# Attention on one core: which VectorE step a cast on GpSimd is tied to, small memsets in front of casts, and a new order of the work

## The chip, the core and the metric

The kernel runs on one core of a Trainium2 chip. The metric is the device time of one execution in microseconds (us). The time before is the median of three runs, 115.96 us (115.36 to 116.09). The engines have short names in the profile: PE is TensorE's matmul, PEld its weight load, DVE is VectorE, ACT is ScalarE, POOL is GpSimd, SP is SyncE, which here only issues DMAs.

## The reference

Softmax attention over 8 batches and 8 heads, 512 queries and keys, 64 columns each, in float32:

```python
q, k, v: (8, 8, 512, 64) float32
scores = einsum('bhqd,bhkd->bhqk', q, k) / sqrt(64)
attn = exp(scores - scores.max(-1)); attn = attn / attn.sum(-1)
return einsum('bhqk,bhkd->bhqd', attn, v)
```

## The kernel before, in words

**The pieces.** Two heads make a pair g (32 pairs, 0 to 31). Three float32 tiles of a pair (q, k and v, 128 partitions by 512 elements, 256 KB each) are loaded by DMA from SP's queue (line 462) into seven buffers of each kind. GpSimd casts each tile to float16: k and q into the tile `qkp` (line 478, five buffers), v into one of twelve tiles `vp` (line 468), which hold a column of ones beside the 64 columns so that the last matmul also gives the row sums. TensorE transposes `qkp` into PSUM (line 502, eight transposes for a pair), and VectorE copies the result to `tqk` in SBUF (line 515). Pairs 0 and 1 go other ways at the start (`first_pair`, and lines 475 to 477 and 508 to 512).

**The groups.** The scores of two blocks of 128 keys by 512 queries make a group m: two matmuls (line 542) into one of three PSUM tiles `st` of 128 by 1024. There are 128 groups, and the last of them is done in two halves. Most groups go to ScalarE, which takes the exponential in one ACTIVATE from `st` to `pt` (line 546). Sixteen groups, listed in `Plan.ON_DVE`, get their exponential on VectorE instead, in six steps: `raise_` (line 566) reads `st` from PSUM and writes a 16-bit whole number `pd`; then five passes in SBUF follow, `pass_` 0 to 4: `m<-pd` (line 583), `pe<-pd` (line 592), the product `m<-m` (line 600), `m<-m` (line 602), and the product `pd<-pd,m` (line 606). The exponential of such a group is the sum of two float16 parts, `pe` and `pd`; TensorE takes the sum in the values' matmuls, which use both as weights.

**The values.** `values` (line 638) multiplies the exponentials by `vp` into a PSUM tile `o` of seven columns of 128 queries each. When a tile is full, VectorE takes the reciprocal of the sums (line 612, `reciprocal`, the plan's step "rec") and multiplies (line 617, `normalise`, the plan's "mul") into a ring in SBUF, from which SP stores (line 628). `last_values` and `finish` end the last head (lines 654, 667, 668, 674).

**Who sets the order.** Each engine works through its own queue in order. Which instruction stands where in each queue is decided before the kernel is built, by the class `Plan`: a small model steps through time, five nanoseconds a step, and for each of PE, DVE, POOL and SP picks the next step by fixed durations and rules. `run` returns the steps sorted by time, and the kernel issues them in that order. The chip is not told of the times; it only sees the order and the semaphores. Rules that matter here:

- `due` (lines 79 to 91) sorts the casts: those of k and q are due `DUEK` before a pair's scores, that of v `DUEV` after them (and `DUEL` later still where a group of the pair is on VectorE). The same order gives the first loads, and a load of pair g+7 follows the cast of pair g.
- `step_pool` (line 118) emits a cast when no pass is at work, or when its due time less `PRE` has come. `step_dve` (line 290) emits casts in front of a VectorE step that is not a pass: up to two before a raise, one before a copy or a normalise, none before a reciprocal. `emit` (line 101) writes the cast down, and from 9000 on (`CALM`) with the flag that it is to be tied.
- Tied means: `cast_behind` (line 489) makes the cast wait on a semaphore for the VectorE instruction that was issued last (`latest[0]`). The steps that `dve` (line 485) records are the raise, the passes, the copy, the reciprocal and the normalise.
- `self.port` is the model's idea of an SBUF port that GpSimd's casts and VectorE's passes share: a pass may not start while a cast holds it (`CAST_PORT`), and a cast not while a pass runs.
- `LATE_NORM`, `LATE_COPY` and `LATE_MUL` bound how far a pass may put off a step of VectorE that will soon be ready; `HURRY`, `SOON` and `BACKLOG` say when PE turns to scores or waits for a PSUM tile, by how much work ScalarE still has.

**Waits of a cast.** A cast of k or q also waits for its DMA, and the one that comes first into a reused `qkp` (the cast of k) for the transposes on TensorE that read the buffer five pairs earlier. An instruction carries few waits; further ones stand before it as instructions of their own in GpSimd's queue.

Of the kernel before, what the change touches and what calls it, by code (L numbers as in the profile page):

```python
# [9 lines left out]
FP32 = mybir.dt.float32  # L10
# [7 lines left out]
class Plan:  # L18
# [15 lines left out]
    STEP = 5  # L34
    CALM, KEEN = 9000, 4
    FIRST_UNIT = 4
    ON_DVE = (5, 9, 19, 22, 35, 40, 50, 53, 63, 73, 78, 85, 92, 100, 109, 120)

    LATE_NORM, LATE_COPY, HURRY, SOON, BACKLOG = 600, 2400, 800, 280, 300
    LATE_MUL, WAIT = 2000, 200  # L40
    SLACK, AHEAD = 0, 2

    CAST, CAST_PORT, CAST_DONE, TO_POOL = 557, 475, 130, 150
    FIRST_LAND, LOAD, STORE, LATENCY, ISSUE = 5200, 740, 370, 2300, 470
    QUEUED, URGENT = 3500, 16
    RAW, QK16, NV, NU = 7, 5, 12, 112
    PAIR, DUEK, DUEV, DUEL, PRE = 3300, 4050, 6000, 6000, 500

    def __init__(self, groups, pairs, first):
        self.groups, self.pairs = groups, pairs  # L50
# [47 lines left out]
    def note(self, t, *what):  # L98
        self.steps.append((t, len(self.steps)) + what)

    def emit(self, t, after):
        _, g, n = self.uncast.pop(0)
        shared = (g, n) == (1, "q")
        self.note(t, "cast", g, n, t > self.CALM)
        if not shared:
            self.casts.append((g, n, t if after is None else after + self.TO_POOL))
        if g + self.RAW < self.pairs:
            self.loads.append((g + self.RAW, n))
# [9 lines left out]
    def step_pool(self, t):  # L118
        if self.uncast and self.uncast[0][1:] != (1, "q") and not self.casts and self.pool <= t:
            quiet = not self.passes and self.port <= t and not any(x[1] == "raise" for x in self.ready)  # L120
            if self.fits(t) and (quiet or self.uncast[0][0] - self.PRE < t):
                self.emit(t, None)
        if self.casts and self.pool <= t and self.port <= t:
            g, n, after = self.casts[0]
            if after <= t and self.landed.get((g, n), 1e9) <= t:
                self.casts.pop(0)
                self.pool = t + self.CAST
                self.port = t + self.CAST_PORT
                self.cast_done[(g, n)] = t + self.CAST + self.CAST_DONE

    def step_sp(self, t):
        if self.sp > t or self.dma > t + self.QUEUED:
# [157 lines left out]
    def step_dve(self, t):  # L290
        if self.uncast and self.uncast[0][1:] == (1, "q"):
            if self.landed.get((1, "q"), 1e9) <= t:
                self.emit(t, None)
                self.dve = t + 240
                self.pool = self.port = t + 330
                self.cast_done[(1, "q")] = t + 400
            return
# [7 lines left out]
        if now:  # L305
# [5 lines left out]
            _, kind, what = job  # L311
            slots = {"raise": 2, "rec": 0}.get(kind, 1)
            while slots and not self.casts and self.fits(t, 60 if slots == 1 else 0):
                self.emit(t, self.dve_done if self.dve_done > t - 300 else None)
                slots -= 1
                if slots and self.fits(t, 500):
                    self.emit(t, self.dve_done if self.dve_done > t - 300 else None)
                    slots -= 1
            self.note(t, kind, *what)
            if kind == "rec":  # L320
# [14 lines left out]
            else:  # L335
# [2 lines left out]
                self.raised.add(what[0])  # L338
                self.passes += [(what[0], s) for s in range(len(self.PASSES))]
                self.passed[what[0], None] = self.dve + self.PASS_DONE  # L340
            self.dve_done = self.dve
        elif self.passes and self.port <= t:
            able = [x for x in self.passes if self.passed.get((x[0], self.NEEDS[x[1]]), 1e9) <= t]
            if not able:
                return
            m, s = able[0]
            end = t + self.PASSES[s]
            late = {
                "copy": self.LATE_COPY,
                "rec": self.LATE_NORM,  # L350
                "mul": self.LATE_MUL,
                "raise": self.LATE_NORM,
                "finish": 0,
            }
            full = len(self.raised) == self.BITS
            if all(x[0] > end - late[x[1]] or (full and x[1] == "raise") for x in self.ready):
                self.passes.remove((m, s))
                self.note(t, "pass", m, s)
                self.dve = self.port = self.dve_done = end
                self.passed[m, s] = end + self.PASS_DONE  # L360
                if s == len(self.PASSES) - 1:
                    self.raised.remove(m)
                    self.exps[m] = end + self.PASS_DONE + self.TO_PE + self.SLACK

    def run(self):
        t = 4600
        self.dve_done = 0
        while self.m < len(self.groups) or self.todo or self.head or self.ready or self.passes or self.stores or self.last_part < 4:
            self.step_sp(t)
            self.step_pool(t)  # L370
# [11 lines left out]
def kernel(  # L382
# [97 lines left out]


    latest = []
    SYNC = mybir.DependencyInfo(mybir.DependencyClass.Sync, mybir.DependencyReason.DATA)

    def dve(ins):
        latest[:] = [ins]
        return ins

    def cast_behind(g, name, behind):
        ins = cast(g, name)  # L490
        if behind and latest:
            tc.add_manual_dep(ins.ins, latest[0].ins.name, SYNC, reason="SBUF ports")

    def transposes(g, n, bank):
        if n == 0:
# [3 lines left out]
            tps[g] = ps_x.tile([P, 2, NI, P], FP16, tag=f"x{bank ^ n}", name=f"tp_{g}_{n}")  # L499
        n = 1 - n  # L500
        for i in range(NI):
            nc.tensor.transpose(tps[g][:, n, i, :], qkp[g][:, n, i, :], ident)  # L502
        if g == 1 and n == 1:
            copy(g, n)

# [328 lines left out]
```

## Time and profile before

| what | value |
|---|---|
| median of three runs | 115.96 us |
| the profiled execution | 115.99 us |
| span of its instructions | 114.2 us |
| granted TensorE clock | 0.998 |
| busy PE / DVE / ACT / POOL | 104.4 / 103.3 / 106.5 / 56.8 us |
| instructions PE / DVE / ACT / POOL | 1687 / 226 / 118 / 101 |
| read and written in HBM | 25.17 MB, 8.39 MB |

The span runs from the first to the last instruction; the 1.8 us between it and the time of the execution lie around it. A group line of the profile gives line, engine, operation, written and read tiles, shapes and count, then busy time and the mean duration of one, then the idle time before. In a timeline a row is start, duration, engine, line, operation, tiles, count; neighbours of one kind are merged into one row. Durations of neighbours on one engine overlap, since the next instruction is taken up while the last one finishes. So an engine's pace is read from start to start.

### The profile page before, as it was taken

How to read it: one execution, taken by the hardware profiler on the slowest of the kernel's cores; microseconds unless marked ns; L12 is line 12 of the kernel's file. 1: busy time of each engine (PE TensorE's matmuls, PEld its weight loads, DVE VectorE, ACT ScalarE, POOL GpSimd, SP SyncE). 2: the span in 40 equal slices, each digit the busy share in tenths (PEclk: the TensorE clock that was granted, in tenths of full speed). 3: DMA queues.
4: the chain of work that ended last, by engine and by line, in shares of the span. 5: the costliest groups of instructions: out<-in, count | busy, mean ns of one | idle time of the engine just before them, and what ended most of it. 6: DMA issues, size and time to landing. Idle time of an engine off the chain costs nothing.

```text
span 114.2 us, 4337 instructions
## 1 busy us (share of the span) xinstructions
PE 104.4 (91%) x1687; PEld 67.9 (59%) x1687; DVE 103.3 (90%) x226; ACT 106.5 (93%) x118; POOL 56.8 (50%) x101
## 2 busy tenths in 40 slices
PE   7966999999999889999999999999999999999950
PEld 2623566566856457666658557567675676577640
DVE  1557899999999999999999999999999999999660
ACT  4698999999999999999999999999999999999940
POOL 2156844785445744784473675655828374400000
PEclk9999999999999999999999999999999999999999
DMA  2899999999999999789899999999995993755243
GB/s 94 277 359 379 384 386 375 384 380 378 384 354 350 354 375 354 259 268 302 216 374 361 305 277 329 326 350 349 366 322 165 301 291 121 260 182 187 98 149 130
DMA packets 35381, 33.84 MB, mean 296 GB/s; under 512 B 2592, under 2 KB 35360, under 8 KB 35360
## 3 DMA queue, kind: packets, MB, share of 16 engines
q1 hardware_dynamic: 34928, 33.17, 87.3%
q10 hardware_dynamic: 432, 0.39, 1.0%
q8 instruction: 13, 0.21, 0.8%
q14 instruction: 8, 0.07, 0.2%
HBM read 25.17 MB, written 8.39 MB: 294 GB/s over the span
## 4 chain that ended last, share of the span: by engine, by line
DVE 50%; PE 20%; DMA 11%; ACT 9%; issue 4%; POOL 1%; SPq 1%; ACTq 0%
PE o L638 10%; DVE pd L566 10%; DVE tqk L515 10%; DVE ring L617 9%; ACT pt L546 9%; PE st L542 8%; DVE m L600 5%; DMA q<-in_q_dram 5%; DVE pd L606 4%; DMA out_dram<-ring 4%; DVE pe L592 3%; DMA v<-in_v_dram 3%; DVE rc L612 2%; DVE m L602 2%; DVE m L583 2%
## 5 line engine op out<-in xcount | busy, mean ns | idle before, releaser
L546 ACT ACTIVATE pt<-st 128x1024 f16<-128x1024 f32 (+1 forms) x110 | 101.3, 1054 | 0.7 <-PE st L542 0.3
L638 PEld LDWEIGHTS <-pt 128*128 128x128 f16 x880 | 38.7, 98 | 13.0 <-issue 10.6
L638 PE MATMUL o<-vp,pt 128*128 128x65 f16 x880 | 45.5, 194 | 0.7 <-DVE ring L617 0.2
L542 PE MATMUL st<-tqk 64*128 64x512 f16 (+1 forms) x250 | 42.5, 381 | 2.2 <-ACT pt L546 0.7
L478 POOL CAST qkp<-k 128x512 f16<-128x512 f32 x31 | 19.1, 616 | 16.5 <-DVE pe L592 4.2
L468 POOL CAST vp<-v 128x512 f16<-128x512 f32 x32 | 19.4, 619 | 14.3 <-DVE m L602 4.3
L478 POOL CAST qkp<-q 128x512 f16<-128x512 f32 x30 | 18.5, 616 | 9.0 <-DVE pe L592 2.4
L638 PE MATMUL o<-vp,pe 128*128 128x65 f16 x128 | 22.2, 195 | 0.2
L617 DVE TENSOR_TENSOR ring<-o,rc 128x448 f32<-128x448 f32 (+2 forms) x37 | 22.1, 599 | 0.1
L638 PE MATMUL o<-vp,pd 128*128 128x65 f16 x128 | 22.0, 193 | 0.1
L502 PEld LDWEIGHTS <-qkp 128*128 128x128 f16 x248 | 14.2, 97 | 10.9 <-issue 5.2
L502 PE MATMUL tp<-ident,qkp 128*128 128x128 f16 x248 | 19.6, 220 | 1.3 <-DVE tqk L515 0.6
L566 DVE TENSOR_SCALAR pd<-st 128x1024 uint16<-128x1024 f32 x16 | 19.4, 1213 | 1.0 <-PE st L542 1.0
L515 DVE COPY tqk<-tp 128x1024 f16<-128x1024 f16 x30 | 20.2, 676 | 0.0
L542 PEld LDWEIGHTS <-tqk 64*128 64x128 f16 x250 | 10.6, 93 | 11.1 <-issue 3.0
L638 PEld LDWEIGHTS <-pe 128*128 128x128 f16 x128 | 12.5, 98 | 2.9 <-issue 2.0
L638 PEld LDWEIGHTS <-pd 128*128 128x128 f16 x128 | 12.6, 98 | 0.4 <-DVE pd L606 0.2
L600 DVE TENSOR_TENSOR m<-m 128x1024 f16<-128x1024 f16 x16 | 12.6, 787 | 0.0
L606 DVE TENSOR_TENSOR pd<-pd,m 128x1024 f16<-128x1024 f16 x16 | 11.8, 739 | 0.0
L612 DVE RECIPROCAL rc<-o 128x7 f32<-128x7 f32 (+2 forms) x37 | 7.1, 192 | 1.3 <-PE o L638 1.3
L592 DVE TENSOR_SCALAR pe<-pd 128x1024 uint16<-128x1024 uint16 x16 | 7.1, 446 | 0.0
L583 DVE TENSOR_SCALAR m<-pd 128x1024 uint16<-128x1024 uint16 x16 | 6.9, 434 | 0.0
(49 smaller groups left out, 31.0 us busy)
## 6 DMA issues: line engine op xcount, KB each, us to landing
v<-in_v_dram SPq DMA_DIRECT2D x32, 256.0 KB, 5.5
k<-in_k_dram SPq DMA_DIRECT2D x31, 256.0 KB, 5.4
q<-in_q_dram SPq DMA_DIRECT2D x31, 256.0 KB, 5.3
out_dram<-ring SPq DMA_DIRECT2D x62, 128.0 KB, 2.9
k<-in_k_dram ACTq DMA_DIRECT2D x2, 128.0 KB, 2.9
q<-in_q_dram SPq DMA_DIRECT2D x2, 128.0 KB, 2.7
out_dram<-ring ACTq DMA_DIRECT2D x1, 128.0 KB, 1.7
out_dram<-obl SPq DMA_DIRECT2D x1, 128.0 KB, 1.7
```

The costliest lines, as they stand in the source:

```text
L468: return nc.gpsimd.tensor_copy(out=vps[g % NV][:, :, :, 0:D], in_=raw[g]["v"][:, :, :, :])
L478: return nc.gpsimd.tensor_copy(out=dst, in_=src[:, :, :, :])
L502: nc.tensor.transpose(tps[g][:, n, i, :], qkp[g][:, n, i, :], ident)
L515: nc.vector.tensor_copy(out=tqk[g][:, :, :], in_=tps.pop(g).rearrange("p n i c -> p n (i c)"))
L542: nc.tensor.matmul(st[:, x, cols], kc, qc[:, cols], start=True, stop=True)
L546: nc.scalar.activation(out=pt[:, :, cols], in_=st[:, :, cols], func=EXP, scale=scale, bias=SHIFT)
L566: nc.vector.tensor_scalar(out=r["pd"][:, :, :], in0=r["st"][:, :, :], scalar1=BITS, scalar2=BIAS, op0=AluOp.mult, op1=AluOp.add,)
L592: ins = nc.vector.tensor_scalar(out=r["pe"][:, :, :], in0=u[:, :, :], scalar1=0x7C00, scalar2=None, op0=AluOp.bitwise_and,)
L600: ins = nc.vector.tensor_tensor(out=m16, in0=m16, in1=m16, op=AluOp.mult)
L606: ins = nc.vector.tensor_tensor(out=u16, in0=u16, in1=m16, op=AluOp.mult)
L617: nc.vector.tensor_tensor(out=ring[:, u % NU : u % NU + n, :], in0=o[:, x : x + n, 0:D], in1=rcs.pop(u)[:, 0:n].broadcast_to([P, n, D]), o ...
L638: nc.tensor.matmul(os[u // 7][:, u % 7, :], part[:, y * P : (y + 1) * P], vps[g % NV][:, h, c, :], start=(n == 0), stop=(n == len(parts) - 1),
```

## The change

The kernel's pieces and their number stay as they are; so does the number of groups on VectorE. What the diff does:

- `trigger` is new. It looks back over VectorE's planned steps (`ops`: start, end, whether it is a pass) over those that follow on without a gap over 20 ns, at most five, to the last pass, and one step further. A cast is now tied to that step, through an index into the list `latest`, which keeps six instructions instead of one.
- In the model a waiting cast begins at the latest of four times (GpSimd free, port free, the tied step's end plus 150 ns, the tile landed), and a pass frees the port before its own end, 265 ns after its start for the single-input passes and 533 ns for the products, where it was the end of the step (333 and 600).
- In front of the cast of k, a memset of one element on GpSimd waits for the transposes that last read the buffer (26 casts, those of pairs 6 to 31).
- Thirteen of the sixteen groups on VectorE are others, and eleven constants of the order are new: `LATE_NORM` 600 to 2300, `LATE_COPY` 2400 to 700, `LATE_MUL` 2000 to 400, `HURRY` 800 to 1000, `SOON` 280 to 200, `BACKLOG` 300 to 700, `DUEK` 4050 to 2800, `DUEV` 6000 to 4000, `DUEL` 6000 to 7000, `PRE` 500 to 0, beside the new port times.

```diff
--- before.py
+++ after.py
@@ -34,17 +34,18 @@
     STEP = 5
     CALM, KEEN = 9000, 4
     FIRST_UNIT = 4
-    ON_DVE = (5, 9, 19, 22, 35, 40, 50, 53, 63, 73, 78, 85, 92, 100, 109, 120)
-
-    LATE_NORM, LATE_COPY, HURRY, SOON, BACKLOG = 600, 2400, 800, 280, 300
-    LATE_MUL, WAIT = 2000, 200
+    ON_DVE = (5, 11, 15, 24, 36, 41, 49, 55, 60, 70, 76, 83, 94, 105, 109, 120)
+
+    LATE_NORM, LATE_COPY, HURRY, SOON, BACKLOG = 2300, 700, 1000, 200, 700
+    LATE_MUL, WAIT = 400, 200
     SLACK, AHEAD = 0, 2
 
     CAST, CAST_PORT, CAST_DONE, TO_POOL = 557, 475, 130, 150
+    SCALE_PORT, PRODUCT_PORT, GAP, REACH = 265, 533, 20, 5
     FIRST_LAND, LOAD, STORE, LATENCY, ISSUE = 5200, 740, 370, 2300, 470
     QUEUED, URGENT = 3500, 16
     RAW, QK16, NV, NU = 7, 5, 12, 112
-    PAIR, DUEK, DUEV, DUEL, PRE = 3300, 4050, 6000, 6000, 500
+    PAIR, DUEK, DUEV, DUEL, PRE = 3300, 2800, 4000, 7000, 0
 
     def __init__(self, groups, pairs, first):
         self.groups, self.pairs = groups, pairs
@@ -98,10 +99,30 @@
     def note(self, t, *what):
         self.steps.append((t, len(self.steps)) + what)
 
-    def emit(self, t, after):
+    def trigger(self, t):
+
+
+
+
+        ops = self.ops
+        if not ops or ops[-1][1] <= t - 300:
+            return 1, None
+        n = len(ops) - 1
+        while (
+            n > 0
+            and len(ops) - n < self.REACH
+            and not ops[n][2]
+            and ops[n][0] - ops[n - 1][1] <= self.GAP
+        ):
+            n -= 1
+        if n > 0 and ops[n][0] - ops[n - 1][1] <= self.GAP:
+            n -= 1
+        return len(ops) - n, ops[n][1]
+
+    def emit(self, t, back, after):
         _, g, n = self.uncast.pop(0)
         shared = (g, n) == (1, "q")
-        self.note(t, "cast", g, n, t > self.CALM)
+        self.note(t, "cast", g, n, back if t > self.CALM else 0)
         if not shared:
             self.casts.append((g, n, t if after is None else after + self.TO_POOL))
         if g + self.RAW < self.pairs:
@@ -119,14 +140,15 @@
         if self.uncast and self.uncast[0][1:] != (1, "q") and not self.casts and self.pool <= t:
             quiet = not self.passes and self.port <= t and not any(x[1] == "raise" for x in self.ready)
             if self.fits(t) and (quiet or self.uncast[0][0] - self.PRE < t):
-                self.emit(t, None)
+                self.emit(t, 1, None)
         if self.casts and self.pool <= t and self.port <= t:
             g, n, after = self.casts[0]
             if after <= t and self.landed.get((g, n), 1e9) <= t:
                 self.casts.pop(0)
-                self.pool = t + self.CAST
-                self.port = t + self.CAST_PORT
-                self.cast_done[(g, n)] = t + self.CAST + self.CAST_DONE
+                begin = max(self.pool, self.port, after, self.landed[(g, n)])
+                self.pool = begin + self.CAST
+                self.port = begin + self.CAST_PORT
+                self.cast_done[(g, n)] = begin + self.CAST + self.CAST_DONE
 
     def step_sp(self, t):
         if self.sp > t or self.dma > t + self.QUEUED:
@@ -290,7 +312,7 @@
     def step_dve(self, t):
         if self.uncast and self.uncast[0][1:] == (1, "q"):
             if self.landed.get((1, "q"), 1e9) <= t:
-                self.emit(t, None)
+                self.emit(t, 1, None)
                 self.dve = t + 240
                 self.pool = self.port = t + 330
                 self.cast_done[(1, "q")] = t + 400
@@ -311,10 +333,11 @@
             _, kind, what = job
             slots = {"raise": 2, "rec": 0}.get(kind, 1)
             while slots and not self.casts and self.fits(t, 60 if slots == 1 else 0):
-                self.emit(t, self.dve_done if self.dve_done > t - 300 else None)
+                behind = self.trigger(t)
+                self.emit(t, *behind)
                 slots -= 1
                 if slots and self.fits(t, 500):
-                    self.emit(t, self.dve_done if self.dve_done > t - 300 else None)
+                    self.emit(t, *behind)
                     slots -= 1
             self.note(t, kind, *what)
             if kind == "rec":
@@ -338,7 +361,7 @@
                 self.raised.add(what[0])
                 self.passes += [(what[0], s) for s in range(len(self.PASSES))]
                 self.passed[what[0], None] = self.dve + self.PASS_DONE
-            self.dve_done = self.dve
+            self.ops.append((t, self.dve, False))
         elif self.passes and self.port <= t:
             able = [x for x in self.passes if self.passed.get((x[0], self.NEEDS[x[1]]), 1e9) <= t]
             if not able:
@@ -356,7 +379,9 @@
             if all(x[0] > end - late[x[1]] or (full and x[1] == "raise") for x in self.ready):
                 self.passes.remove((m, s))
                 self.note(t, "pass", m, s)
-                self.dve = self.port = self.dve_done = end
+                self.dve = end
+                self.ops.append((t, end, True))
+                self.port = t + (self.SCALE_PORT if self.PASSES[s] == self.SCALE else self.PRODUCT_PORT)
                 self.passed[m, s] = end + self.PASS_DONE
                 if s == len(self.PASSES) - 1:
                     self.raised.remove(m)
@@ -364,7 +389,7 @@
 
     def run(self):
         t = 4600
-        self.dve_done = 0
+        self.ops = []
         while self.m < len(self.groups) or self.todo or self.head or self.ready or self.passes or self.stores or self.last_part < 4:
             self.step_sp(t)
             self.step_pool(t)
@@ -480,16 +505,23 @@
 
 
     latest = []
+    reads = {}
+    mark = cpool.tile([P, 1], FP32, name="mark")
     SYNC = mybir.DependencyInfo(mybir.DependencyClass.Sync, mybir.DependencyReason.DATA)
 
     def dve(ins):
-        latest[:] = [ins]
+        latest[:] = [ins] + latest[: Plan.REACH]
         return ins
 
     def cast_behind(g, name, behind):
+
+
+        if name == "k" and g - Plan.QK16 in reads:
+            small = nc.gpsimd.memset(mark[0:1, :], 0.0)
+            tc.add_manual_dep(small.ins, reads[g - Plan.QK16].ins.name, SYNC, reason="tile")
         ins = cast(g, name)
         if behind and latest:
-            tc.add_manual_dep(ins.ins, latest[0].ins.name, SYNC, reason="SBUF ports")
+            tc.add_manual_dep(ins.ins, latest[behind - 1].ins.name, SYNC, reason="SBUF ports")
 
     def transposes(g, n, bank):
         if n == 0:
@@ -499,7 +531,7 @@
             tps[g] = ps_x.tile([P, 2, NI, P], FP16, tag=f"x{bank ^ n}", name=f"tp_{g}_{n}")
         n = 1 - n
         for i in range(NI):
-            nc.tensor.transpose(tps[g][:, n, i, :], qkp[g][:, n, i, :], ident)
+            reads[g] = nc.tensor.transpose(tps[g][:, n, i, :], qkp[g][:, n, i, :], ident)
         if g == 1 and n == 1:
             copy(g, n)
 
```

## The prediction

> **What bounds the kernel now.** I read the page's head and its costliest group first, then the sums of one long stretch, then ScalarE's timeline for its pace, then VectorE's passes.
>
> ```profile
> span 114.2 us, 4337 instructions
> PE 104.4 (91%) x1687; PEld 67.9 (59%) x1687; DVE 103.3 (90%) x226; ACT 106.5 (93%) x118; POOL 56.8 (50%) x101
> L546 ACT ACTIVATE pt<-st 128x1024 f16<-128x1024 f32 (+1 forms) x110 | 101.3, 1054 | 0.7 <-PE st L542 0.3
> ```
> ```profile
> core 0: us, PE busy (x) PEld busy (x) DVE busy (x) ACT busy (x) POOL busy (x), PEclk, DMA share, GB/s
> 9.17:109.74 100.57, 96.80 (x1636) 64.21 (x1632) 98.54 (x199) 100.22 (x109) 53.60 (x91) 1.00 0.92 307
> ```
>
> From 9.17 to 109.74 us ScalarE is busy for 100.22 of 100.57 us. VectorE (98.54) and TensorE (96.80) are nearly full beside it, and the clock is 1.00. ScalarE does the same number of exponentials before and after, since sixteen groups stay on VectorE, so only its waits can go. The idle column shows 0.7 us, but neighbours overlap, which hides short waits. The pace shows them:
>
> ```profile
> 9.17 100.57 ACT L546 ACTIVATE pt<-st 128x1024 f16<-128x1024 f32 x109 [0.34 <-PE st L542]
> 14.61 12.08 ACT L546 ACTIVATE pt<-st 128x1024 f16<-128x1024 f32 x13
> 25.47 1.22 ACT L546 ACTIVATE pt<-st 128x1024 f16<-128x1024 f32 x1
> 108.66 1.08 ACT L546 ACTIVATE pt<-st 128x512 f16<-128x512 f32 x2
> ```
>
> The second and third row are an undisturbed stretch: 13 activations, the last of 1.22 us, so (12.08 - 1.22) / 12 = 0.905 us from start to start. Of the 109 in the first row 107 are full ones, and the two halves at the end start at 108.66. At that pace 107 steps take 96.8 us, and they took 108.66 - 9.17 = 99.49 us. So 2.65 us of waits lie inside ScalarE's stretch, and this is all that a better order can win there. What lies ahead of 9.17 us hangs on the first loads, and what lies behind 109.74 us is the last head's normalisation and store; I leave both as they are.
>
> Starting each activation from the one before, I find twenty waits over 25 ns behind the row at 9.17, 2.8 us together. (Rounding makes this 0.2 more than 2.65.) Nine of them, 1.05 us together, come within 1.3 us behind a VectorE pass that took over 60 ns more than the shortest of its kind. The first and the last of the nine:
>
> ```profile
> 25.47 3.05 ACT L546 ACTIVATE pt<-st 128x1024 f16<-128x1024 f32 x3
> 27.34 1.19 ACT L546 ACTIVATE pt<-st 128x1024 f16<-128x1024 f32 x1
> 25.61 0.59 DVE L592 TENSOR_SCALAR pe<-pd 128x1024 uint16<-128x1024 uint16 x1
> 84.26 2.90 ACT L546 ACTIVATE pt<-st 128x1024 f16<-128x1024 f32 x3
> 84.46 0.92 DVE L606 TENSOR_TENSOR pd<-pd,m 128x1024 f16<-128x1024 f16 x1
> ```
>
> From 25.47 to 27.34 are two steps, 1.87 us instead of 1.81: 0.06 lost behind a pass of 0.59 us. The last of the three from 84.26 starts about 1.02 us before their end, which again makes 1.87 us for two. The other eleven, 1.8 us, have no such pass near them.
>
> **The change: casts at the port.** How long the passes take is seen in their shortest, median and longest:
>
> ```profile
> L600 DVE TENSOR_TENSOR m<-m x16: 633/777/1033, 14.4 to 104.5; 128x1024 f16<-128x1024 f16 x16
> L606 DVE TENSOR_TENSOR pd<-pd,m x16: 640/706/921, 16.6 to 106.1; 128x1024 f16<-128x1024 f16 x16
> L592 DVE TENSOR_SCALAR pe<-pd x16: 369/412/615, 13.7 to 104.2; 128x1024 uint16<-128x1024 uint16 x16
> L583 DVE TENSOR_SCALAR m<-pd x16: 369/414/589, 11.1 to 103.3; 128x1024 uint16<-128x1024 uint16 x16
> L602 DVE TENSOR_SCALAR m<-m x16: 369/422/501, 16.0 to 105.3; 128x1024 f16<-128x1024 f16 x16
> L600 DVE TENSOR_TENSOR m<-m 128x1024 f16<-128x1024 f16 x16 | 12.6, 787 | 0.0
> L606 DVE TENSOR_TENSOR pd<-pd,m 128x1024 f16<-128x1024 f16 x16 | 11.8, 739 | 0.0
> L592 DVE TENSOR_SCALAR pe<-pd 128x1024 uint16<-128x1024 uint16 x16 | 7.1, 446 | 0.0
> L583 DVE TENSOR_SCALAR m<-pd 128x1024 uint16<-128x1024 uint16 x16 | 6.9, 434 | 0.0
> L602 DVE TENSOR_SCALAR m<-m 128x1024 f16<-128x1024 f16 x16 | 6.7, 417 | 0.0
> ```
>
> Mean less shortest, times 16: 2.5 us at line 600, 1.6 at 606, 1.2 at 592, 1.0 at 583, 0.8 at 602: some 7 us in which a pass only stands. What it stands for is a cast:
>
> ```profile
> 30.03 0.37 DVE L592 TENSOR_SCALAR pe<-pd 128x1024 uint16<-128x1024 uint16 x1
> 30.32 0.61 DVE L617 TENSOR_TENSOR ring<-o,rc 128x448 f32<-128x448 f32 x1
> 30.86 0.92 DVE L600 TENSOR_TENSOR m<-m 128x1024 f16<-128x1024 f16 x1
> 30.62 0.62 POOL L478 CAST qkp<-k 128x512 f16<-128x512 f32 x1 [1.50 <-DVE pe L592]
> 31.82 0.42 DVE L602 TENSOR_SCALAR m<-m 128x1024 f16<-128x1024 f16 x1
> 32.69 0.77 DVE L606 TENSOR_TENSOR pd<-pd,m 128x1024 f16<-128x1024 f16 x1
> 32.30 0.62 POOL L478 CAST qkp<-q 128x512 f16<-128x512 f32 x1 [1.07 <-DVE m L602]
> ```
>
> The pass ends at 30.40, the cast of k tied to it starts 0.22 us later, and the product at 30.86 takes 0.92 instead of 0.63 us. The cast of q at 32.30 starts 0.06 us behind its pass (32.24), and the product behind it takes 0.77. By POOL's timeline 12 casts of k start about 0.22 us behind their pass and some 30 of q and v about 0.06. The extra 0.16 of k is its further waits, one after the other in the queue; with the memset taking TensorE's wait ahead of time, k should go as q goes.
>
> What a cast gains that already stands at the port is shown by one pair of rows alone, before the casts are tied:
>
> ```profile
> 7.33 0.29 DVE L476 CAST qkp<-q 128x256 f16<-128x256 f32 x1 [0.94 <-DMA q<-in_q_dram]
> 7.36 0.52 POOL L477 CAST qkp<-q 128x256 f16<-128x256 f32 x1 [0.38 <-DMA q<-in_q_dram]
> L702 POOL CAST k<-k 128x128 f16<-128x128 f32 x1 | 0.4, 379 | 2.2 <-DMA k<-in_k_dram 2.2
> L478 POOL CAST qkp<-k 128x512 f16<-128x512 f32 x31 | 19.1, 616 | 16.5 <-DVE pe L592 4.2
> ```
>
> A cast of 256 elements alone would take about 379 + (616 - 379) / 3 = 0.46 us (an estimate from the rows of 128 and 512). At 7.36 it starts while a VectorE cast runs and takes 0.52, ending 0.26 us behind that cast (7.62). So some 0.20 us of it had been done beside the other. For a full cast this gives an end 0.20 + 0.06 = 0.26 us earlier than now for q and v, and 0.42 for k. The product at 30.86 ended at 31.78; less its shortest time, 0.63, it got the port at 31.15, 0.53 us after the cast began. A waiting cast would leave the port 0.53 + 0.06 - 0.26 = 0.33 us behind the pass, and the normalise between (0.54 from 30.32 to 30.86) covers that. Bounds: nothing gained (0) and all 7 us; I take 5 of VectorE's 7 us, because casts that follow one another behind one step still collide. These 5 us are not on the path by themselves: VectorE loses its queue of work, and ScalarE gets what hung on it.
>
> In the Trainium skill the page "SBUF — State Buffer", section "Who interferes with whom", calls the shared port pair an exclusive lock for the whole instruction, and its section "A bandwidth-pool intuition that's wrong (but worth ruling out)" gives "blocked until DVE-end + ~115 ns". By that figure a waiting cast would start 0.05 us later than q and v do now; the rows at 7.33 and 7.36 speak against it.
>
> **The memsets.** Twenty-six on GpSimd:
>
> ```profile
> 0.24 0.10 POOL L818 MEMSET const-float32-0.0<- 128x1 f32 x1 [0.24 <-issue]
> 0.27 0.10 POOL L818 MEMSET const-float32-1.0<- 128x1 f32 x1
> ```
>
> The pace is 0.03 us, 26 x 0.03 = 0.9 us of POOL, which is idle for half of the span: nothing on the path. No row shows a memset beside a pass. Bounds: nothing, or each holds a pass for its 0.10 us, 2.6 us of VectorE; I take nothing, since it waits for transposes of five pairs ago and comes right behind the cast before it. If that cover is gone, it eats half of the 5 us. What queues behind it on POOL is only the cast that waited for the same transposes already.
>
> **The order.** `LATE_NORM` and `LATE_COPY` stay above the 0.6 us of the longest pass and cost nothing: a pass is only weighed against steps still to come. `LATE_MUL` 400 keeps a product from standing between a reciprocal and its normalise: at most 0.12 us of idle VectorE each, and the normalise frees its PSUM tile earlier; I set both at nothing together. `SOON` 200 and `BACKLOG` 700 let TensorE stand up to 0.2 us for scores, a gain for ScalarE. `DUEK`, `DUEV` and `PRE` move casts of k and q later against those of v, 1.25 us and 2 us; in the first loads v of pair 0 goes ahead of k and q of pair 3. The later loads, on SP's queue behind later casts, have seven buffers, over 20 us, against
>
> ```profile
> k<-in_k_dram SPq DMA_DIRECT2D x31, 256.0 KB, 5.4
> ```
>
> so they are hidden. What a later cast of k can cost is a rival below. Thirteen new places on VectorE do not change the work. The tail keeps its last VectorE group (120) and its steps.
>
> **Sum.** Profiled execution 115.99 us, 0.03 above the median. Off: the nine waits, 1.05 us. Off: of the other 1.8 us a fifth, 0.35, as raises start sooner on a VectorE that is no longer full. Added: nothing. 115.99 - 1.4 = 114.6 us. Ends: 115.99 - 2.65 = 113.3 if all waits go, and 116.0 if none does.
>
> **Rivals.**
> 1. Nearly all waits go. For it: PE and VectorE both get slack. Against: in eleven waits no stretched pass stands near. Time: 2.65 less a tenth, 113.6 us.
> 2. VectorE gets free and nobody uses it. ScalarE's waits come from the order of scores and three `st` tiles. For it: those eleven waits. Time: only 0.2 us off, 115.8.
> 3. The change does not do what it says: a cast at the port gets under way only when the pass is over, as late as q and v now. Then only the 12 casts of k gain, 0.16 us each, 1.9 of VectorE's 7 us, and of the 1.05 us 0.3 go: 115.7 us. For it: no row shows a full cast waiting. Against: the rows at 7.33. By the Trainium skill's figure above, k would gain 0.10 and each of the 30 others lose 0.05, 1.2 against 1.5 us of VectorE, which makes about 116.0.
> 4. Slower: casts of k and q come too late. Transposes already stand for casts now:
>
> ```profile
> PEld L502 <- POOL qkp L478: 4.0, 12, 0.5
> ```
>
> Twelve times, 0.33 us each, still covered by the filled `st` tiles. With k and q 1.25 us later, each of 31 pairs can lose time on ScalarE. From 1.4 / 31 = 0.045 us a pair on, the gain is gone; from 0.08 on it is over 1% slower. At 0.09 us: 114.6 + 2.8 = 117.4 us. Against: the model lays the casts out with these waits in it.
>
> **How the numbers follow.** Chances: forecast 0.46 (its own range 114.0 to 115.2), rival 1 0.14, rival 2 0.13, rival 3 0.06, rival 4 0.21. A measurement of this kernel tells about 1%, that is 1.2 us, from no change. Faster by over 1% means under 114.8: rival 1 and three quarters of the forecast's case, 0.14 + 0.35 = 0.49. Within 1%: the rest of the forecast, 0.11, rivals 2 and 3, and a little of rival 4 (0.01), 0.31. Slower: 0.20. The range 113.5 to 117.0 leaves out the lower edge of rival 1 and the worse half of rival 4.
>
> **What would show it.** Right: casts longer than 616 ns in the mean (they wait inside), starting before the end of a pass; lines 600 and 606 near 640, the single-input passes near 370; VectorE with idle time between 20 and 100 us; ScalarE's stretch below 99.4 us. Wrong: passes as long as now (rival 3); VectorE idle but ScalarE's stretch near 100.5 (rival 2); larger waits of line 502 for line 478 and gaps in ScalarE behind them (rival 4); memsets standing beside stretched passes.

## The result, and the profile after

| | before | after |
|---|---|---|
| median of 20 runs (us) | 115.86 (115.27 to 116.47) | 114.86 (114.28 to 115.68) |
| ratio, with 95% interval | 1 | 0.9926 (0.9908 to 0.9944) |
| the profiled execution (us) | 115.99 | 114.75 |
| its span (us) | 114.2 | 113.0 |

The change makes the kernel 0.74% faster, 0.56 to 0.92%. The forecast was 114.6 us. Its largest chance, 0.49, was for faster by over 1%; what came is within 1%, to which it gave 0.31. The time lies in the range, and the gain, 1.0 us between the medians, is smaller than the 1.4 us forecast.

The head of the page after, its first group, and ScalarE's timeline (the row from 7.84 on, then the second activation of it, which is the kernel's fourth, like the one at 9.17 before, and the two halves at the end):

```profile
span 113.0 us, 4341 instructions
PE 103.8 (92%) x1687; PEld 68.9 (61%) x1687; DVE 101.4 (90%) x226; ACT 105.6 (93%) x118; POOL 64.9 (57%) x127
L578 ACT ACTIVATE pt<-st 128x1024 f16<-128x1024 f32 (+1 forms) x110 | 100.4, 1096 | 0.0
```
```profile
7.84 100.39 ACT L578 ACTIVATE pt<-st 128x1024 f16<-128x1024 f32 x110
8.78 1.03 ACT L578 ACTIVATE pt<-st 128x1024 f16<-128x1024 f32 x1
107.03 1.21 ACT L578 ACTIVATE pt<-st 128x512 f16<-128x512 f32 x2
```

The 107 full steps from the fourth activation to the first half take 107.03 - 8.78 = 98.25 us; before, from 9.17 to 108.66, they took 99.49. So 1.24 of the 2.65 us of waits are gone. The span is 1.23 us shorter (these two executions lie 1.24 us apart, the medians 1.00), but it is not that simple. Ahead of these steps 0.39 us came off, which I do not count: the start of this stretch moved between 8.65 and 9.53 us in the runs below, among kernels with the same first steps too. Behind them 0.40 us was added: from the first half to the end of the span it is 113.0 - 107.03 = 5.95 us now and was 114.2 - 108.66 = 5.55.

VectorE's five passes, shortest, median and longest:

```profile
L632 DVE TENSOR_TENSOR m<-m x16: 676/682/689, 12.0 to 102.9; 128x1024 f16<-128x1024 f16 x16
L638 DVE TENSOR_TENSOR pd<-pd,m x16: 676/682/703, 14.7 to 104.5; 128x1024 f16<-128x1024 f16 x16
L624 DVE TENSOR_SCALAR pe<-pd x16: 374/418/569, 11.6 to 102.6; 128x1024 uint16<-128x1024 uint16 x16
L615 DVE TENSOR_SCALAR m<-pd x16: 372/418/504, 11.0 to 101.7; 128x1024 uint16<-128x1024 uint16 x16
L634 DVE TENSOR_SCALAR m<-m x16: 374/417/428, 13.2 to 103.7; 128x1024 f16<-128x1024 f16 x16
```

All 32 products take 0.68 to 0.70 us, where before they went up to 1.03. No cast holds a product up any more; two single-input passes, of 0.57 and 0.50 us, still stand behind one. The casts themselves, GpSimd's rows and one waiting cast beside VectorE's steps:

```profile
L503 POOL CAST qkp<-k x31: 599/615/1007, 5.8 to 89.8; 128x512 f16<-128x512 f32 x31
L503 POOL CAST qkp<-q x30: 603/700/1011, 8.5 to 90.5; 128x512 f16<-128x512 f32 x30
L520 POOL MEMSET mark<- x26: 88/88/90, 16.4 to 89.8; 1x1 f32 x26
```
```profile
45.97 0.42 DVE L615 TENSOR_SCALAR m<-pd 128x1024 uint16<-128x1024 uint16 x1
46.30 0.69 DVE L638 TENSOR_TENSOR pd<-pd,m 128x1024 f16<-128x1024 f16 x1
46.45 1.01 POOL L503 CAST qkp<-q 128x512 f16<-128x512 f32 x1 [0.86 <-DVE m L615]
```

The cast starts at 46.45, 0.06 us behind the step ahead (46.39), and finds the product at work. It takes 1.01 us and ends at 47.46, 0.47 us behind the product's end (46.99). A cast tied to the pass itself ended 0.06 + 0.62 = 0.68 us behind it. So a wait at the port saves 0.21 us, and for a cast of k 0.37 (0.22 + 0.62 before). This is the mechanism the change was made for, and it works: 38 casts of the trace start inside a pass, 23 of them inside a single-input pass and 15 inside a product, and 37 of the 38 end 0.47 to 0.49 us behind it.

The Trainium skill, page "SBUF — State Buffer", section "Who interferes with whom", says of a VectorE instruction in a two-port mode that whoever issues first gets the shared pair for the whole instruction and the other "fully blocks". The trace agrees that the cast waits, behind both kinds of pass, but what follows the wait is 0.47 us instead of a whole cast of 0.62.

### The profile page after: what moved, and what is told of

Read it like the earlier page. It is cut to its first block, busy times and chain, and to the rows that moved or that the text cites. A ratio compares the mean times of both kernels' runs of the same rounds, so it can differ in the third digit from the quotient of the medians.

```text
span 113.0 us, 4341 instructions
## 1 busy us (share of the span) xinstructions
PE 103.8 (92%) x1687; PEld 68.9 (61%) x1687; DVE 101.4 (90%) x226; ACT 105.6 (93%) x118; POOL 64.9 (57%) x127
## 4 chain that ended last, share of the span: by engine, by line
PE 45%; DVE 42%; ACT 7%; issue 2%
PE o L670 19%; PE st L574 15%; DVE pd L598 9%; DVE tqk L547 8%; DVE ring L649 7%; PE tp L534 7%; ACT pt L578 7%; DVE m L632 4%; DVE pd L638 3%; PE st_0a L717 3%; DVE pe L624 2%; DVE m L615 2%; DVE m L634 2%; DVE rc L644 2%; PE st L760 1%
## 5 line engine op out<-in xcount | busy, mean ns | idle before, releaser
L670 PE MATMUL o<-vp,pt 128*128 128x65 f16 x880 | 46.3, 194 | 0.2
L503 POOL CAST qkp<-k 128x512 f16<-128x512 f32 x31 | 21.5, 693 | 11.6 <-DMA k<-in_k_dram 5.2
L493 POOL CAST vp<-v 128x512 f16<-128x512 f32 x32 | 21.7, 696 | 7.9 <-DVE rc L644 2.6
L503 POOL CAST qkp<-q 128x512 f16<-128x512 f32 x30 | 21.3, 710 | 6.7 <-DVE rc L644 3.3
L574 PEld LDWEIGHTS <-tqk 64*128 64x128 f16 x250 | 11.6, 93 | 11.7 <-issue 4.3
L638 DVE TENSOR_TENSOR pd<-pd,m 128x1024 f16<-128x1024 f16 x16 | 10.9, 683 | 0.0
L632 DVE TENSOR_TENSOR m<-m 128x1024 f16<-128x1024 f16 x16 | 10.9, 683 | 0.0
```

Of the source, the lines that this page charges most:

```text
L493: return nc.gpsimd.tensor_copy(out=vps[g % NV][:, :, :, 0:D], in_=raw[g]["v"][:, :, :, :])
L503: return nc.gpsimd.tensor_copy(out=dst, in_=src[:, :, :, :])
L574: nc.tensor.matmul(st[:, x, cols], kc, qc[:, cols], start=True, stop=True)
L632: ins = nc.vector.tensor_tensor(out=m16, in0=m16, in1=m16, op=AluOp.mult)
L638: ins = nc.vector.tensor_tensor(out=u16, in0=u16, in1=m16, op=AluOp.mult)
L670: nc.tensor.matmul(os[u // 7][:, u % 7, :], part[:, y * P : (y + 1) * P], vps[g % NV][:, h, c, :], start=(n == 0), stop=(n == len(parts) - 1),
```

## The experiments

Ten kernels were run. The theory: what the change gains is the time that passes stand behind casts, on a VectorE that has no idle time, and the tie to the step ahead takes it out. The rivals: the new order carries the gain; or VectorE's freed time is used by nobody. Each kernel was compared with runs of the kernel before on the same chip. The table gathers what each trace gives: the sum of the 80 passes (16 times the five mean durations), ScalarE's 107 steps (from the fourth activation to the first half, as above), and the rest of the span from that half on. These three columns come from one execution of each kernel, and the 20 times of the kernel before alone spread over 1.2 us, so a difference of a few tenths between two rows shows little by itself.

| kernel | order | tie | memsets | ratio (95%) | passes, us | 107 steps, us | rest, us |
|---|---|---|---|---|---|---|---|
| before | old | last step | no | 1 | 45.2 | 99.49 | 5.55 |
| b_memset | old | last step | yes | 0.9904 (0.9869 to 0.9940) | 43.3 | 98.52 | 5.56 |
| b_tie_ahead | old | step ahead | no | 0.9914 (0.9886 to 0.9942) | 41.3 | 98.23 | 5.55 |
| b_tie_memset | old | step ahead | yes | 0.9913 (0.9884 to 0.9942) | 41.9 | 98.21 | 5.57 |
| a_order_alone | new | last step | no | 1.0166 (1.0124 to 1.0208) | 44.9 | 101.29 | 5.80 |
| a_tie_last | new | last step | yes | 1.0058 (1.0036 to 1.0080) | 43.5 | 99.85 | 5.80 |
| a_no_memset | new | step ahead | no | 0.9958 (0.9934 to 0.9983) | 42.3 | 98.68 | 5.77 |
| after | new | step ahead | yes | 0.9926 (0.9908 to 0.9944) | 41.8 | 98.25 | 5.95 |

**a_tie_last**, the changed kernel with the old tie:

```diff
-            tc.add_manual_dep(ins.ins, latest[behind - 1].ins.name, SYNC, reason="SBUF ports")
+            tc.add_manual_dep(ins.ins, latest[0].ins.name, SYNC, reason="SBUF ports")
```

> The changed kernel with its order and its memsets, but each cast tied to VectorE's last step again instead of the step ahead of the last pass. If the port wait carries the gain: no cast starts inside a pass, casts take 0.62 us again, products go from 0.68 back to 0.75 us or more in the mean, and the time goes back to about that of the kernel before, ratio 0.998 to 1.005. If the new order carries it: the same stretched passes, but the ratio stays near 0.993.

Measured: 1.0058. All casts take 0.60 to 0.62 us again, no longer starting inside a pass, and the whole gain is gone. The new order with memsets is slower than the kernel before, by 0.4 to 0.8%. Products are at 0.69 and 0.71 in the mean, less than the 0.75 expected; the pass `pe<-pd` stands more than in the kernel before (463 ns in the mean beside 446):

```profile
L638 DVE TENSOR_TENSOR pd<-pd,m 128x1024 f16<-128x1024 f16 x16 | 11.4, 711 | 0.0
L632 DVE TENSOR_TENSOR m<-m 128x1024 f16<-128x1024 f16 x16 | 11.0, 690 | 0.0
L624 DVE TENSOR_SCALAR pe<-pd 128x1024 uint16<-128x1024 uint16 x16 | 7.4, 463 | 0.0
```

**a_no_memset**, the changed kernel without its memsets:

```diff
-        if name == "k" and g - Plan.QK16 in reads:
-            small = nc.gpsimd.memset(mark[0:1, :], 0.0)
-            tc.add_manual_dep(small.ins, reads[g - Plan.QK16].ins.name, SYNC, reason="tile")
```

> The changed kernel without the 26 memsets, so that the casts of k wait for the transposes themselves. If a cast at the port hides its other waits under the pass: ratio to the kernel before 0.992 to 0.995, as with memsets. If the memsets carry a part of their own: casts of k start 0.16 us later, products behind them stand again, ratio 0.996 or more.

Measured: 0.9958, its interval overlaps both cases and that of the change. The trace has 107 steps of 98.68 us against 98.25, so the memsets may be worth some 0.4 us in this order; the ratio alone does not settle it.

**b_tie_ahead**, the kernel before with its steps and their order kept, and the tie alone changed (`trigger` as in the change, but only to choose the instruction):

```diff
-                self.emit(t, self.dve_done if self.dve_done > t - 300 else None)
+                self.emit(t, self.dve_done if self.dve_done > t - 300 else None, self.trigger(t)[0])
...
-            tc.add_manual_dep(ins.ins, latest[0].ins.name, SYNC, reason="SBUF ports")
+            tc.add_manual_dep(ins.ins, latest[behind - 1].ins.name, SYNC, reason="SBUF ports")
```

> The kernel before with its order kept step for step, and only the tie changed: each cast waits for the step ahead of the last pass. If the port wait carries the gain: products at 0.68 to 0.70 us in the mean, some 3 us less of VectorE's time, ratio 0.993 to 0.997. If the order carries it, or VectorE's freed time is used by nobody: the same shorter passes, ratio 0.998 to 1.002.

Measured: 0.9914. Products at 0.68 and 0.69 in the mean, as expected, and all of the gain without the new order:

```profile
L624 DVE TENSOR_TENSOR m<-m 128x1024 f16<-128x1024 f16 x16 | 11.0, 685 | 0.0
L630 DVE TENSOR_TENSOR pd<-pd,m 128x1024 f16<-128x1024 f16 x16 | 10.9, 679 | 0.0
```

**b_tie_memset**, the same with the 26 memsets:

```diff
+        if name == "k" and g - Plan.QK16 in reads:
+            small = nc.gpsimd.memset(mark[0:1, :], 0.0)
+            tc.add_manual_dep(small.ins, reads[g - Plan.QK16].ins.name, SYNC, reason="tile")
         ins = cast(g, name)
...
-            nc.tensor.transpose(tps[g][:, n, i, :], qkp[g][:, n, i, :], ident)
+            reads[g] = nc.tensor.transpose(tps[g][:, n, i, :], qkp[g][:, n, i, :], ident)
```

> The kernel before in its own order with the tie to the step ahead of the last pass and the 26 memsets, so all of the change but the new order. Port wait: ratio 0.992 to 0.996, all products at 0.68 us. Order: 0.998 to 1.002 with the same passes.

Measured: 0.9913. With these two the rival "the order carries it" falls: old order and new order end at the same time, within the intervals, once the other two parts are in.

**a_order_alone**, both edits of a_tie_last and a_no_memset at once:

```diff
-        if name == "k" and g - Plan.QK16 in reads:
-            small = nc.gpsimd.memset(mark[0:1, :], 0.0)
-            tc.add_manual_dep(small.ins, reads[g - Plan.QK16].ins.name, SYNC, reason="tile")
...
-            tc.add_manual_dep(ins.ins, latest[behind - 1].ins.name, SYNC, reason="SBUF ports")
+            tc.add_manual_dep(ins.ins, latest[0].ins.name, SYNC, reason="SBUF ports")
```

> The new order alone: casts tied to VectorE's last step, no memsets. The new order with the old tie and memsets gave 1.0058. If memsets matter only through the tie: 1.004 to 1.008 here too. If the memsets help casts of k that are tied to the last step (0.16 us each): 1.008 to 1.015.

Measured: 1.0166, above what I expected if memsets matter only through the tie. The new order by itself (thirteen other groups and ten new constants) costs 1.2 to 2.1%. Not because its passes stand longer: their sum, 44.9 us, is a little below the 45.2 of the kernel before, and yet ScalarE's 107 steps take 1.80 us more. In this order the standing costs more: from here to the whole change 3.1 us come off the passes (44.9 to 41.8) and 3.04 off the steps. Why is not shown. One thing that differs is that TensorE's transposes wait a little longer for casts of k and q, 4.7 us beside 4.0 in the kernel before:

```profile
PEld L531 <- POOL qkp L503: 4.7, 12, 0.7
```

Added to this order alone, the memsets take back 1.1% (a_tie_last) and the tie 2.1% (a_no_memset); both together take back 2.4%.

**b_memset**, the kernel before with the memsets alone (the edit of b_tie_memset on the kernel before, its tie kept):

```diff
+        if name == "k" and g - Plan.QK16 in reads:
+            small = nc.gpsimd.memset(mark[0:1, :], 0.0)
+            tc.add_manual_dep(small.ins, reads[g - Plan.QK16].ins.name, SYNC, reason="tile")
         ins = cast(g, name)
         if behind and latest:
             tc.add_manual_dep(ins.ins, latest[0].ins.name, SYNC, reason="SBUF ports")
```

> The kernel before with the 26 memsets alone, its order and its tie kept. If the further waits of a cast of k cost something: 12 casts start 0.16 us earlier, some 1 to 2 us less of standing in the passes behind them, ratio 0.995 to 0.998. If they cost nothing on ScalarE, or a memset stands in the way of passes: 0.999 to 1.003.

Measured: 0.9904. This I had not expected: 26 memsets, most of 0.09 us (four take 0.37), give the old order as much as the tie does. VectorE's and GpSimd's timelines show how (the pass `pe<-pd` that the cast of k is tied to, the step between, the product behind):

```profile
30.11 0.37 DVE L597 TENSOR_SCALAR pe<-pd 128x1024 uint16<-128x1024 uint16 x1
30.40 0.61 DVE L622 TENSOR_TENSOR ring<-o,rc 128x448 f32<-128x448 f32 x1
30.93 0.77 DVE L605 TENSOR_TENSOR m<-m 128x1024 f16<-128x1024 f16 x1
30.55 0.61 POOL L478 CAST qkp<-k 128x512 f16<-128x512 f32 x1 [1.32 <-DMA q<-in_q_dram]
```

The cast of k starts 0.07 us behind its pass, not 0.22, and the product behind takes 0.77 us instead of the 0.92 of the same place before. Eleven casts of k start 0.06 to 0.07 us behind their pass now. Pass by pass, 0.77 of the 1.83 us by which the passes' sum falls (45.2 to 43.3) come at passes that a cast of k held: nine are shorter by 0.08 to 0.17 us, 1.22 together, and two are longer, 0.45 together. The other 1.06 us come at casts of q and v. Three of the five largest of these follow right behind a cast of k in GpSimd's queue and so are earlier with it; for the rest the cause is open. Earlier transposes are not what was won: they wait for casts of k and q 4.7 us here and 4.0 before.

Now the sums can be laid side by side in the old order. The first 1.8 us taken from the passes shorten ScalarE's stretch by 0.97 us. The next 1.4 to 2.0 (b_tie_memset, b_tie_ahead) give 0.3 more, and the ratios, 0.9904, 0.9913 and 0.9914, not even that. In b_tie_ahead VectorE gets idle instead: its busy time between 10 and 100 us, in the kernel before, in b_memset, in b_tie_ahead:

```profile
10.00:100.00 90.00, 86.23 (x1423) 56.55 (x1421) 89.58 (x180) 89.75 (x99) 52.83 (x90) 1.00 0.97 323
```
```profile
10.00:100.00 90.00, 87.05 (x1457) 57.55 (x1457) 89.40 (x182) 89.92 (x100) 54.13 (x116) 1.00 1.01 322
```
```profile
10.00:100.00 90.00, 86.83 (x1462) 57.99 (x1460) 88.15 (x182) 90.00 (x100) 57.64 (x90) 1.00 0.98 328
```

The third number behind the 90.00 is VectorE's: 89.58, 89.40, 88.15 us. The fourth is ScalarE's: 89.75, 89.92, 90.00. So VectorE's further time is used by nobody, as far as the ratios can tell.

**b_no_tie**, the kernel before without any tie:

```diff
-        if behind and latest:
-            tc.add_manual_dep(ins.ins, latest[0].ins.name, SYNC, reason="SBUF ports")
```

> The kernel before in its order without any tie: a cast runs as soon as GpSimd comes to it and its data are there. If it is the place of the casts that counts: casts meet passes at random, some win the port, passes stand more than before, ratio 1.00 to 1.02. If it is enough that a cast is at the port early, whatever it meets: 0.990 to 0.997, as with the tie to the step ahead.

Measured: 1.0808 (1.0754 to 1.0862), worse than expected. Casts and passes take turns at the port:

```profile
32.97 0.83 DVE L581 TENSOR_SCALAR m<-pd 128x1024 uint16<-128x1024 uint16 x1
33.83 0.71 DVE L590 TENSOR_SCALAR pe<-pd 128x1024 uint16<-128x1024 uint16 x1
35.00 1.11 DVE L598 TENSOR_TENSOR m<-m 128x1024 f16<-128x1024 f16 x1
36.15 0.72 DVE L600 TENSOR_SCALAR m<-m 128x1024 f16<-128x1024 f16 x1
```
```profile
32.45 1.07 POOL L468 CAST vp<-v 128x512 f16<-128x512 f32 x1
33.47 0.80 POOL L478 CAST qkp<-k 128x512 f16<-128x512 f32 x1
34.22 0.80 POOL L478 CAST qkp<-q 128x512 f16<-128x512 f32 x1
34.96 0.61 POOL L478 CAST qkp<-k 128x512 f16<-128x512 f32 x1
35.52 1.07 POOL L478 CAST qkp<-q 128x512 f16<-128x512 f32 x1
```

Every pass here takes 1.6 to 2 times what it takes alone (0.68 the products, 0.42 the others), since the next cast is at the port when the last pass ends. The passes' sum is 54.8 us, the 107 steps 109.4. It is not enough to be early; a cast has to wait behind the last pass before a step that leaves the port alone. (The normalise of seven columns is such a step: in the kernel before, 29 of them beside a cast take 0.57 to 0.62 us, and six without one 0.62 to 0.63.)

**a_17_groups**, the changed kernel with a seventeenth group on VectorE and seven other constants of the order:

```diff
-    ON_DVE = (5, 11, 15, 24, 36, 41, 49, 55, 60, 70, 76, 83, 94, 105, 109, 120)
+    ON_DVE = (5, 12, 18, 27, 34, 39, 45, 53, 59, 70, 76, 84, 89, 96, 106, 113, 121)
...
-    LATE_NORM, LATE_COPY, HURRY, SOON, BACKLOG = 2300, 700, 1000, 200, 700
+    LATE_NORM, LATE_COPY, HURRY, SOON, BACKLOG = 2300, 700, 800, 100, 100
...
-    PAIR, DUEK, DUEV, DUEL, PRE = 3300, 2800, 4000, 7000, 0
+    PAIR, DUEK, DUEV, DUEL, PRE = 3300, 3400, 5000, 6000, 250
```

> The changed kernel with a seventeenth group on VectorE and an order made for it (seventeen places and some constants are new). If VectorE's freed time can be used: one activation of 0.9 us less on ScalarE against some 3.3 us more on VectorE, ratio to the kernel before 0.983 to 0.990. If VectorE is full again with it and ScalarE waits for what it lost: 0.993 to 1.003.

Measured: 0.9974 (0.9944 to 1.0004), no better than the change. One full activation is gone, but the stretch of 106 steps takes 97.69 us (9.15 to 106.84), only 0.56 less than the 107 of the change, and from the first half to the end of the span it takes 113.66 - 106.84 = 6.82 us instead of 5.95. The last group on VectorE, 121, ends late: its last product ends 0.66 us behind ScalarE's first half, and its values are left for the end. Whether seventeen groups with a better end would win stays open.

**b_late_qv**, the kernel before with four memsets between the tied step and each tied cast of q or v:

```diff
+        if behind and latest and name != "k":
+            for n in range(4):
+                small = nc.gpsimd.memset(mark[0:1, :], 0.0)
+                if n == 0:
+                    tc.add_manual_dep(small.ins, latest[0].ins.name, SYNC, reason="late")
         ins = cast(g, name)
```

> The kernel before, with four small memsets on GpSimd put between the tied step and each tied cast of q or v, so that these some 30 casts start about 0.15 us later, as late as those of k. If late casts cost time through the passes behind them, whichever tile they make: 30 x 0.15, some 3 to 4.5 us more of standing on a VectorE that has no idle time, ratio 1.012 to 1.035. If only the casts of k matter, since transposes and scores hang on them: 0.999 to 1.006.

Measured: 1.1082 (1.1038 to 1.1126). The dose was wrong. The memsets write the same element in turn and each waits for the one before, 0.15 us a step, 28.8 us of GpSimd in all, so that TensorE's transposes waited for GpSimd too. The run tells nothing of what it was made for; the next one gives each of the four memsets an element of its own.

**b_late_qv_small**:

```diff
-                small = nc.gpsimd.memset(mark[0:1, :], 0.0)
+                turn[0] += 1
+                small = nc.gpsimd.memset(marks[turn[0] % 16][0:1, :], 0.0)
```

> As the run before with four small memsets ahead of the tied casts of q and v, but each into a byte of its own, so that they do not wait for one another: in the run before each waited 0.15 us for the last, which held 61 casts up by some 0.4 us and GpSimd by 29 us in all. Now a cast should start 0.12 to 0.16 us later. If a late start costs time through the passes behind it: 30 x 0.15, up to 4.5 us of standing, of which by the gain of the memsets alone (12 x 0.16 = 1.9 us gave 1.1 us) about 0.6 is seen: 2 to 3 us, ratio 1.015 to 1.025. If only the casts of k matter: 0.999 to 1.006.

Measured: 1.0601 (1.0569 to 1.0634). One tied cast, with the pass ahead and the product behind it, and the products' rows:

```profile
29.16 0.42 DVE L610 TENSOR_SCALAR m<-m 128x1024 f16<-128x1024 f16 x1
30.63 1.05 DVE L614 TENSOR_TENSOR pd<-pd,m 128x1024 f16<-128x1024 f16 x1
29.84 0.60 POOL L468 CAST vp<-v 128x512 f16<-128x512 f32 x1
30.53 0.60 POOL L468 CAST vp<-v 128x512 f16<-128x512 f32 x1
L608 DVE TENSOR_TENSOR m<-m 128x1024 f16<-128x1024 f16 x16 | 14.6, 913 | 0.0
L614 DVE TENSOR_TENSOR pd<-pd,m 128x1024 f16<-128x1024 f16 x16 | 13.1, 819 | 0.0
```

The first cast starts 0.26 us behind its pass (29.58), the second follows, and the product behind takes 1.05 us. The passes' sum rises by 6.8 us (45.2 to 52.0) and ScalarE's 107 steps by 7.0 (99.49 to 106.49). So "only the casts of k matter" falls. What was added to the passes of a full VectorE comes out about one for one here, as in b_no_tie (9.6 us on the passes, 9.9 on the steps). Some of it may go by TensorE, which waits more for GpSimd here (6.1 us for the memsets and 2.3 for casts of k and q, beside 4.0 before); the two were not parted.

## Why the prediction was right, and where it was not

- **ScalarE bounds, and 2.65 us can be won.** Right: 1.24 us came off its 107 steps, against a forecast of 1.4; the two agree by more than the reasons deserve, as the next points show, and that is luck.
- **Seven us of standing passes, five of them taken.** Mis-sized. "Mean less shortest" took 633 ns for an undisturbed product and 369 for a single-input pass. After the change all 32 products take 676 or more with nothing in their way, and the single-input passes 0.41 to 0.42 us in the mean. The four products of before under 0.65 us all stand right behind a reciprocal, and after the change no product does, so they were no measure for the others. By the medians after, 80 undisturbed passes take 41.9 us, so the standing was 45.2 - 41.9 = 3.3 us, and in the sum nearly all of it went.
- **What a waiting cast gains.** Forecast 0.26 us for q and v and 0.42 for k; measured 0.21 and 0.37. The one pair of rows at 7.33 and 7.36 was a good guide, and rival 3 falls. The ~115 ns that the prediction set against it stand in the Trainium skill (page "SBUF — State Buffer", section "A bandwidth-pool intuition that's wrong (but worth ruling out)") for a DMA whose descriptors GpSimd writes, not for a cast.
- **Nine waits near stretched passes, 1.05 us.** The sum held by chance, the attribution did not. First, the twenty waits are 2.33 us by the unrounded starts, not 2.8: the nine 1.04, the other eleven 1.29 instead of 1.8 (the rest of the 2.65 us lies in waits under 25 ns). In b_tie_ahead, with the same order, the nine places still wait 0.40 us together and so gave 0.64; the other eleven, which I had given 0.35, gave 0.68 (1.29 to 0.61), and four waits at new places cost 0.26. A pass that stands makes later steps of a full VectorE late, so its cost may show further on than 1.3 us; this fits, but no run shows it.
- **Memsets at nothing.** Right as a cost in the changed kernel, where each of the 26 starts behind the cast ahead of it and takes 0.09 us. Wrong as the price of the part: alone in the old order they give 0.6 to 1.3%. I had seen the 0.16 us by which casts of k were late, but counted it under the tie; in the old order either part alone gives the whole gain, and the second adds nothing that can be told.
- **The order at nothing.** Wrong in parts, right in the sum by cover: alone it costs 1.66%, and with both other parts it is not faster than the old order (0.9926 beside 0.9913).
- **"The tail keeps its last VectorE group (120) and its steps."** Failed: 0.40 us were added behind the first half. In the table the kernels with the new order have 5.77 to 5.95 us there, those with the old 5.55 to 5.57. VectorE's last reciprocal of seven columns, before and after:

```profile
108.96 0.20 DVE L612 RECIPROCAL rc<-o 128x7 f32<-128x7 f32 x1 [0.89 <-PE o L638]
```
```profile
107.55 0.21 DVE L644 RECIPROCAL rc<-o 128x7 f32<-128x7 f32 x1 [0.89 <-PE o L670]
```

  In both it waits for TensorE's values. It comes 0.30 us behind ScalarE's first half before (108.66) and 0.52 after (107.03): 0.22 of the 0.40. This belongs to the order and not to the shorter time, since a_order_alone, whose 107 steps take longest of the eight, has it at 0.53 us, and the old order with its steps as short as now (98.21, b_tie_memset) keeps 0.30. The other 0.18 us, in the change alone, lie at the last store: it is issued 0.05 us and lands a further 0.13 us later. Why was not tried.

- **Rivals.** Rival 2 is half of the truth: in the old order VectorE's freed time beyond the first 1.8 us is used by nobody. Rival 4 did not come: TensorE's transposes wait less for GpSimd now, 2.6 us instead of 4.0:

```profile
PEld L534 <- POOL mark L520: 1.3, 4, 0.5
PEld L534 <- POOL qkp L503: 1.3, 4, 0.4
```

- What stays open is where the other 1.4 us of ScalarE's waits come from. They are there in both orders with undisturbed passes.

## What to carry to other kernels

Where two engines share a port, tie the work of the one to an earlier step of the other, so that it already waits at the port when the other's last use ends; and do so only where a step follows that leaves the port alone. Look at every wait that stands between the release and the work: in the old order 26 instructions of 0.09 us that took a wait ahead of time were worth as much as the new tie. Price parts that cure the same thing together, since their gains do not add, and try a new order by itself: here it cost 1.7%. And what a microsecond of standing costs depends on the order and on how much is left: about one for one in the new order and in the runs that added standing, half of it for the first 1.8 us taken from the old order, and next to nothing behind that.

## What the runs showed of the hardware

- A cast of 512 elements that waits at the port ends 0.47 us behind the pass that held it, one that is released behind the pass 0.68: about 0.15 us of its own 0.62 runs beside the pass.
- The other way round it is the same: in b_no_tie 22 single-input passes start inside a cast and end 0.28 us behind it (one takes 0.42 alone), and 14 products end 0.54 us behind it (0.68 alone).
- A memset of one element on GpSimd stands as well when it meets a single-input pass. In b_tie_memset two of the 26 took 0.37 us, like this one, which ends 0.03 us behind the pass (GpSimd's row, then VectorE's):

```profile
15.81 0.37 POOL L517 MEMSET mark<- 1x1 f32 x1
15.72 0.43 DVE L631 TENSOR_SCALAR m<-m 128x1024 f16<-128x1024 f16 x1
```

- Four memsets on GpSimd follow one another at 0.03 us when each writes its own element, and at 0.15 us when they write the same one.
